# Feed-forward weight tiles loaded block by block into two lasting buffers, and one ordering tie taken out

## The chip, the cores and the metric

The kernel runs on one core of one Trainium2 chip. The metric is the device time of one execution, in microseconds; the time of a kernel is the median of several executions. The profile comes from one further execution that was recorded by the hardware profiler.

## The reference, cut to what matters

One step of a streaming encoder: a convolution layer and an attention layer, each followed by a SwiGLU feed-forward block. Only the two feed-forward blocks are touched by the change. For 640 rows (512 prompt frames and 8 x 16 sample frames), width 1024 and hidden width 2816, each computes

```python
def swiglu_ffn(h, g, w_in, w_out):
    a, b = jnp.split(rms_norm(h, g) @ w_in, 2, axis=-1)
    return h + (jax.nn.silu(a) * b) @ w_out
```

All numbers are float32; the matrix products have to be accurate to about that.

## The kernel before, in words

**Precision.** Every operand x of a product is split into a rounded part "hi" (an ACT copy, line 375) and a rest "lo" (a DVE subtraction, line 376). A product is three matmuls: hi x hi, lo x hi, hi x lo (`product`, line 437, with the matmul on line 444). In the text such a pair of copy and subtraction is a "cut".

**Seven products for eight.** The 640 columns are worked on as two halves of 320, and a weight tile as four blocks. Most tiles (22 inner tiles of a feed-forward block less the first three, and all 12 tiles of the output chunks) replace the eight block products by seven, of sums of blocks (a Strassen scheme). The seven weight operands are called X11, X21, XT2, XT1, XT3, XT4, X22.

**One weight tile** is prepared in `w_seven` (line 414). It takes a buffer `raw` (128 partitions x 2048 floats) from `wraw()` (line 382), which allocates a new tile of a pool with two buffers at each call, so a buffer is free again when everything that touched its last tile is done. One DMA on SP's queue loads the whole tile (line 418): 1024 KB for an inner tile (`w_in`, four blocks of 512 columns), 768 KB for an output tile (`w_os`, four blocks of 384). In the buffer the blocks stand in the order a12, a11, a21, a22, numbered 0 to 3 below. Beside it POOL's queue loads a21 into a small buffer `s1` and then a22 with an accumulating DMA (lines 421 and 422), so that s1 = a21 + a22. Then, in this order for an inner tile:

- X11 is cut from a11, and X21 from a12;
- two DVE sums in place, a21 = a11 + a21 (line 429) and a11 = s1 + a11 (line 430), then XT2 is cut from a11;
- XT1 is cut from s1, XT3 from a21, XT4 from a22;
- a12 = a12 + a11 on DVE (line 432), then X22 is cut from a12.

For an output tile the order is XT1, X11, X21, XT2, X22, XT3, XT4. Each cut goes into one of 11 slots that are taken in turn (line 393), so it waits until the matmuls of the cut eleven places earlier are done.

**The order of the work.** The program is handed to a scheduler, which puts each engine's instructions into a fixed order ahead of time, by priority and its own timeline; at run time each engine works strictly in that order and waits where a semaphore says so. `tc.issue_after(i)` (in the helper `behind`, line 140) forces an instruction behind `i` on the same engine. `w_seven` uses it with `late`: all cuts and sums but those listed in `soon` are put behind the instructions in `late`.

**`seven`** (line 535) does one inner tile: it calls `w_seven`, then the products X11, X21, XT2, XT1, XT3 of this tile, with XT4 and X22 of the tile ahead between them (`before(0)`, `before(1)`). The product X11 is copied out of its accumulator by ACT (`keep`, line 456) before XT2 accumulates on top of it. The list `tile_end` holds the last DVE subtraction of the tile ahead, and is handed to `w_seven` as part of `late` with `soon=(X11, X21, XT1)`: so this tile's sums and its cuts XT2, XT3, XT4, X22 stand behind the last cut of the tile ahead. `chunk_add` does the same with the last addition to h of an output chunk.

**One feed-forward block** (`ffn`, line 337): three inner tiles in the plain way (`w_std`, line 398, which also takes its buffers from `wraw()` and loads them in two DMAs, line 406); then three rounds of inner tiles (3, then 6, then 6) with an output chunk of 4 tiles after each (`out_chunk`, line 568; the order of its products is written out by hand in `QORD`); then four inner tiles; then the rest of the output weights (line 711). The stretch of tiles that go through `w_seven` lasts from about 285 to 625 us in the first block and from about 1050 to 1386 us in the second.

Of the kernel before, what the change touches and what calls it, by code (L numbers as in the profile page):

```python
# [8 lines left out]
F32 = mybir.dt.float32  # L9
# [6 lines left out]
P = 128  # L16
# [44 lines left out]
X11, X21, XT2, XT1, XT3, XT4, X22 = range(7)  # L61
# [24 lines left out]
def tile_trunk(ctx, tc, xT, vecs, hist, w_pw1, w_pw2, w_in0, w_out0, w_os0, w_in1, w_out1, w_os1,  # L86
               w_kq, w_v, w_o, rel, kc, vc, y_out, convp_out, convs_out, k_out, v_out):
    nc = tc.nc

    cst = ctx.enter_context(tc.tile_pool(name="cst", bufs=1))  # L90
    wp = ctx.enter_context(tc.tile_pool(name="wp", bufs=2))
# [12 lines left out]
    def nm(s):  # L104
        uid[0] += 1
        return f"{s}_{uid[0]}"

    def mmt(n=512):
        return mm.tile([P, n], F32, tag="mm", name=nm("mm"))
# [29 lines left out]
    @contextmanager  # L139
    def behind(*ins):  # L140
        with ExitStack() as st:
            for i in ins:
                st.enter_context(tc.issue_after(i))
            yield
# [192 lines left out]
    def ffn(l, w_in, w_out, w_os, tail, hf, lead=(), b0=None, last_sum=()):  # L337
# [19 lines left out]
        lead, put_end = list(lead), [None, None]  # L357

        def ties():
            return lead.pop(0) if lead else ()  # L360
# [13 lines left out]
        def put(hi, lo, src):  # L374
            put_end[1] = nc.scalar.activation(out=hi, in_=src, func=AF.Copy).ins  # L375
            put_end[0] = nc.vector.tensor_tensor(out=lo, in0=src, in1=hi.bitcast(F32), op=sub).ins  # L376

        def cut(w, o, src):
            c = slice(o, o + src.shape[-1])
            put(w[0][:, c], w[1][:, c], src)  # L380

        def wraw():
            return wp.tile([P, 2048], F32, tag="raw", name=nm("raw"))

        wbig = [[wp.tile([P, 2048], F32R, tag="w" + t, name=nm("w" + t)) for t in ("hi", "lo")]
                for _ in range(2)]
# [6 lines left out]
        def slot():  # L393
            turn[0] += 1
            hi, lo, o = slots[(turn[0] - 1) % len(slots)]
            return (hi, lo), o

        def w_std(src, small):
            raw = wraw()
            if small:  # L400
                ws = [slot() for _ in range(3)]
                ws.append(([two(i).rearrange("p a n -> p (a n)") for i in (12, 13)], 0))
            else:
                ws = [slot() for _ in range(4)]
            for i in range(0, 2048, 1024):
                nc.sync.dma_start(raw[:, i:i + 1024], src[:, i:i + 1024])
                with tc.high_priority(offset=HP):
                    n = 512 if small else 1024
                    for j in range(i, i + 1024, n):
                        with behind(*ties()):  # L410
                            cut(*ws[j // 512], raw[:, j:j + n])
            return ws[1], ws[0], ws[2], ws[3]

        def w_seven(src, out=False, first=(), rest=(), late=(), soon=()):
            n = src.shape[-1] // 4
            raw, ws = wraw(), {}
            s1 = wx.tile([P, 512], F32, tag="s1", name=nm("s1"))[:, :n]
            nc.sync.dma_start(raw[:, :4 * n], src)
            a12, a11, a21, a22 = (raw[:, n * i:n * i + n] for i in range(4))
            with tc.high_priority(offset=HP), behind(*ties()):  # L420
                nc.gpsimd.dma_start(s1, src[:, 2 * n:3 * n])  # L421
                nc.gpsimd.dma_start(s1, src[:, 3 * n:4 * n], accum_op=add)
                for x in ((XT1, X11, X21, XT2, X22, XT3, XT4) if out else
                          (X11, X21, XT2, XT1, XT3, XT4, X22)):
                    ws[x] = slot()
                    with behind(*(() if x in soon else late),
                                *(first if x == XT1 else rest)):
                        if x == XT2:
                            nc.vector.tensor_tensor(out=a21, in0=a11, in1=a21, op=add)
                            nc.vector.tensor_tensor(out=a11, in0=s1, in1=a11, op=add)  # L430
                        elif x == X22:
                            nc.vector.tensor_tensor(out=a12, in0=a12, in1=a11, op=add)
                        cut(*ws[x], {XT1: s1, X11: a11, X21: a12, XT2: a11, X22: a12,
                                     XT3: a21, XT4: a22}[x])
            return ws
# [12 lines left out]
        def xproduct(pt, w, x, first):  # L448
            return product(pt, w, [(XH[x][:, k, :], XL[x][:, k, :]) for k in range(4)], first)
# [3 lines left out]
        def keep(tag, pt):  # L453
            t = tp.tile([P, NH], F32, tag=tag, name=nm(tag))
            with tc.high_priority(offset=HP):
                keeps.append(nc.scalar.activation(out=t, in_=pt, func=AF.Copy).ins)  # L456
            return t

        def plus(t, pt):
            with tc.high_priority(offset=HP):  # L460
                nc.vector.tensor_tensor(out=t, in0=pt, in1=t, op=add)

        def silu(t, src):
            with tc.high_priority(offset=HP):
                nc.scalar.activation(out=t, in_=src, func=AF.Silu)  # L465
# [60 lines left out]
                        own(XT4, b21)  # L526
            return sink

        xt2_end, xt3_end, chunk_add, tile_end = [], [None], [], []

        def tie(own):
            xt2_end.append(own)
            return {2: xt2_end[:1], 3: xt2_end[2:]}.get(len(xt2_end), ())

        def seven(src, sink, before):
            ws = w_seven(src, late=chunk_add[:1] + tile_end, soon=(X11, X21, XT1))
            chunk_add[:1], tile_end[:] = (), put_end[:1]
            pa, pb = mmt()[:, :NH], mmt()[:, :NH]
            xproduct(pa, ws[X11], X11, True)
            t1 = keep("t1", pa)  # L540
            before(0)
            xproduct(pb, ws[X21], X21, True)
            plus(t1, pb)
            silu(t1, t1)
            before(1)
            own = xproduct(pa, ws[XT2], XT2, False).ins
            t2 = keep("t2", pa)
            pe = mmt()[:, :NH]
            with behind(*tie(own)):
                xproduct(pe, ws[XT1], XT1, True)  # L550
            xt3_end[0] = xproduct(pa, ws[XT3], XT3, False).ins
            t3 = keep("t3", pa)
            plus(t3, pe)

            def after(i):
                if i == 0:
                    last = xproduct(pa, ws[XT4], XT4, False)
                    sink(0, t1, pa)
                else:
                    last = xproduct(pe, ws[X22], X22, False)  # L560
                    plus(t2, pe)
                    silu(t2, t2)
                    sink(1, t2, t3)
                return last

            return after
# [126 lines left out]
        for c in range(NCH):  # L693
            for jj in range(NSTD if c == 0 else 0, CW):
                if jj % 2 == 0:
                    held = [None] * 3
                if jj == NSTD and c == 0:
                    held = helds[1]
                after = seven(w_in[CW * c + jj], combined(HH, HL, jj // 2, jj % 2, held, True),
                              after)  # L700
            after = out_chunk(c, HH, HL, after)
            HH, HL = {}, {}
        hids = [(two(2 * jj), two(2 * jj + 1)) for jj in range(FT - NCH * CW)]
        for jj, hid in enumerate(hids):
            after = seven(w_in[NCH * CW + jj], plain(hid), after)
# [3 lines left out]
        for m0 in (0, 4):  # L709
            raw, w = wraw(), wbig[m0 // 4]  # L710
            nc.sync.dma_start(raw.rearrange("p (m c) -> p m c", m=4),
                              w_out[m0:m0 + 4].rearrange("m p c -> p m c"))
            with tc.high_priority(offset=HP):
                for o in range(0, 2048, 1024):
                    cut(w, o, raw[:, o:o + 1024])
            done += [(m0 + i, [(w[0][:, b:b + P], w[1][:, b:b + P])
                               for b in range(512 * i, 512 * i + 512, P)]) for i in range(4)]
# [419 lines left out]
    for _ in ffn(0, w_in0, w_out0, w_os0, GR, hf, last_sum=last_sum)[1]:  # L1137
        pass
# [454 lines left out]
    for p in range(NP):  # L1593
# [8 lines left out]
        for op in BO[p].split():  # L1602
# [11 lines left out]
            i = int(op[1]) if len(op) > 1 else None  # L1614
# [25 lines left out]
    adds, late = [], []  # L1640
# [28 lines left out]
    for i in range(SPREAD_AT, KT):  # L1669
        with tc.issue_after(end):  # L1670
# [4 lines left out]

    hf = ExitStack()
    spare, products = ffn(1, w_in1, w_out1, w_os1, ((256, 384), (0, 256)), hf,
                                     [(split_end[0], i) for i in (adds[1], adds[3], eps_end, eps_end)] +
                                     [(eps_end,)],
# [190 lines left out]
```

## Time and profile before

| | us |
|---|---|
| median of 3 runs | 1433.54 |
| lowest, highest | 1432.31, 1435.24 |
| the profiled execution | 1431.13 |
| its span, first to last instruction | 1429.4 |

Engines in the profile: PE is the matrix engine and PEld its loading of weights, which runs beside the matmul ahead; DVE, ACT and POOL are the vector, scalar and general engines; SP issues most DMAs. Their busy times in the span: DVE 1110.7 us, ACT 746.2 us, POOL 280.1 us. A row of the waits names who waited, for whom, the time in total, how often, and the longest. In the rows of instruction groups and of the timeline the brackets or the last columns give the engine's idle time just before, and what ended it. A DMA's row in the chain of waits lasts from its issue until the waiting engine goes on.

### The profile page before, as it was taken

How to read it: one execution, taken by the hardware profiler on the slowest of the kernel's cores; microseconds unless marked ns; L12 is line 12 of the kernel's file. 1: busy time of each engine (PE TensorE's matmuls, PEld its weight loads, DVE VectorE, ACT ScalarE, POOL GpSimd, SP SyncE). 2: the span in 40 equal slices, each digit the busy share in tenths (PEclk: the TensorE clock that was granted, in tenths of full speed). 3: DMA queues.
4: the chain of work that ended last, by engine and by line, in shares of the span. 5: the costliest groups of instructions: out<-in, count | busy, mean ns of one | idle time of the engine just before them, and what ended most of it. 6: DMA issues, size and time to landing. Idle time of an engine off the chain costs nothing.

```text
span 1429.4 us, 28234 instructions
## 1 busy us (share of the span) xinstructions
PE 1416.8 (99%) x11076; PEld 1364.3 (95%) x11076; DVE 1110.7 (78%) x2490; ACT 746.2 (52%) x1633; POOL 280.1 (20%) x335
## 2 busy tenths in 40 slices
PE   9999999999999999999999999999999999999998
PEld 9998799999999999999998988888999999999998
DVE  6799767998888888765666757667899788798765
ACT  5666554554563564545654544544564564465453
POOL 5799120011111111012111111110011111111101
PEclk9999999999999999999999999999999999999999
DMA  7257424054544543524456555561134544543522
GB/s 253 88 168 192 123 84 145 16 137 122 164 112 119 137 123 108 154 89 174 165 187 207 182 185 173 181 215 36 59 99 131 154 127 111 134 131 103 138 86 74
DMA packets 66932, 192.57 MB, mean 135 GB/s; under 512 B 12144, under 2 KB 30320, under 8 KB 58480
## 3 DMA queue, kind: packets, MB, share of 16 engines
q1 hardware_dynamic: 52432, 160.58, 34.4%
q0 software_dynamic: 13504, 29.37, 10.2%
q8 instruction: 87, 1.43, 0.4%
q10 hardware_dynamic: 864, 0.83, 0.2%
q14 instruction: 45, 0.37, 0.1%
HBM read 179.14 MB, written 11.61 MB: 133 GB/s over the span
## 4 chain that ended last, share of the span: by engine, by line
PE 92%; DVE 4%; DMA 1%; ACT 1%; issue 1%; POOL 0%; DVEq 0%; ACTq 0%; POOLq 0%
PE mm L444 51%; PE mm L1304 11%; PE mm L202 6%; PE mm L204 6%; PE mm L203 6%; PE mm L916 3%; PE w L1304 2%; PE am L1477 1%; PE am L1549 1%; PE am L1493 1%; PE w L1448 1%; PE w L1511 1%; DMA raw<-in_w_in 1%; PE mm L149 1%; PE w L243 1%
## 5 line engine op out<-in xcount | busy, mean ns | idle before, releaser
L444 PE MATMUL mm<-XH,whi 128*128 128x320 f32 x896 | 276.2, 310 | 1.3 <-ACT t L456 1.3
L444 PE MATMUL mm<-XH,wlo 128*128 128x320 f32 x896 | 276.5, 309 | 0.0
L444 PE MATMUL mm<-XL,whi 128*128 128x320 f32 x896 | 274.9, 309 | 0.0
L375 ACT ACTIVATE whi<-raw 128x512 fp32r<-128x512 f32 (+2 forms) x280 | 166.7, 613 | 147.4 <-PE mm L444 80.9
L376 DVE TENSOR_TENSOR wlo<-raw,whi 128x512 fp32r<-128x512 f32 (+2 forms) x280 | 185.1, 671 | 23.0 <-ACT whi L375 21.8
L444 PEld LDWEIGHTS mm<-XH,whi 128*128 128x128 f32 x896 | 167.9, 188 | 3.3 <-ACT t L456 3.3
L444 PE MATMUL mm<-hid,whi 128*128 128x320 f32 x732 | 170.9, 310 | 0.2 <-DVE hid L376 0.2
L444 PEld LDWEIGHTS mm<-XH,wlo 128*128 128x128 f32 x896 | 168.2, 188 | 0.0
L444 PEld LDWEIGHTS mm<-XL,whi 128*128 128x128 f32 x896 | 167.8, 188 | 0.0
L202 PE MATMUL mm<-xh,whi 128*128 128x320 f32 (+2 forms) x416 | 128.9, 313 | 0.8 <-DVE h L726 0.4
L203 PE MATMUL mm<-xh,wlo 128*128 128x320 f32 (+2 forms) x416 | 128.1, 310 | 0.0
L444 PEld LDWEIGHTS mm<-hid,whi 128*128 128x128 f32 x732 | 124.7, 188 | 1.8 <-DVE h L595 0.8
L204 PE MATMUL mm<-xl,whi 128*128 128x320 f32 (+2 forms) x416 | 125.5, 310 | 0.0
L595 DVE TENSOR_TENSOR h<-h,mm 128x320 f32<-128x320 f32 x168 | 79.5, 486 | 44.4 <-PE mm L444 44.3
L444 PE MATMUL mm<-hid,wlo 128*128 128x320 f32 x366 | 113.1, 309 | 0.0
L444 PE MATMUL mm<-XH,shi 128*128 128x320 f32 x344 | 105.9, 310 | 0.7 <-DVE h L1581 0.7
L444 PE MATMUL mm<-XH,slo 128*128 128x320 f32 x344 | 106.0, 308 | 0.0
L444 PE MATMUL mm<-XL,shi 128*128 128x320 f32 x344 | 105.7, 309 | 0.0
L872 POOL TENSOR_TENSOR ca<-ca,cvt 128x512 f32<-128x512 f32 x60 | 89.7, 1494 | 15.0 <-ACT cvt L869 8.8
L375 ACT ACTIVATE shi<-raw 128x512 fp32r<-128x512 f32 (+1 forms) x114 | 65.9, 586 | 49.6 <-PE mm L444 21.7
L421 POOL DMA_DIRECT2D s<-in_w_in x38 | 22.0, 580 | 330.4 <-ACT t L465 67.3
L202 PEld LDWEIGHTS mm<-xh,whi 128*128 128x128 f32 x416 | 78.0, 188 | 3.3 <-ACT xh L190 1.5
(337 smaller groups left out, 3662.6 us busy)
## 6 DMA issues: line engine op xcount, KB each, us to landing
raw<-in_w_in SPq DMA_DIRECT2D x38, 1024.0 KB
s<-in_w_in POOLq DMA_DIRECT2D x76, 256.0 KB, 4.2
raw<-in_w_os SPq DMA_DIRECT2D x24, 768.0 KB
cache<-in_ck SPq DMA_DIRECT2D x32, 512.0 KB
cache<-in_cv SPq DMA_DIRECT2D x32, 512.0 KB
raw<-in_w_pw SPq DMA_DIRECT2D x11, 1024.0 KB
s<-in_w_os POOLq DMA_DIRECT2D x48, 192.0 KB, 3.7
raw<-in_w_kq SPq DMA_DIRECT2D x8, 1024.0 KB
```

The lines of the kernel that those rows point to most:

```text
L149: end = nc.tensor.matmul(pt[:, 0:P], ident, ident, start=True, stop=True)
L202: nc.tensor.matmul(ps, wh, xh, start=(first and i == 0), stop=False)
L203: nc.tensor.matmul(ps, wl, xh, start=False, stop=False)
L204: end = nc.tensor.matmul(ps, wh, xl, start=False, stop=(stop and i == last))
L375: put_end[1] = nc.scalar.activation(out=hi, in_=src, func=AF.Copy).ins
L376: put_end[0] = nc.vector.tensor_tensor(out=lo, in0=src, in1=hi.bitcast(F32), op=sub).ins
L421: nc.gpsimd.dma_start(s1, src[:, 2 * n:3 * n])
L444: last = nc.tensor.matmul(pt, wt, v, start=(first and k == i == 0), stop=(k == n - 1 and i == 2), skip_group_check=True)
L595: hadd[i, u] = [nc.vector.tensor_tensor(out=hv, in0=hv, in1=pt, op=sub if row else add).ins]
L872: nc.gpsimd.tensor_tensor(out=acc, in0=acc, in1=pr, op=ALU.add)
L916: conv_end[0] = nc.tensor.matmul(pt[32 * q:32 * q + 32, 0:n], w4[0:r, 4 * tg + q, :], mv, start=(tg == 0), stop=(tg == 7)).ins
L1304: step_end[0] = nc.tensor.matmul(ps, w, x, start=i == j == 0, stop=i == len(wts) - 1 and j == 2).ins
```

## The change

Three things, all in `ffn`:

- Two buffers `raw` are allocated once for the whole feed-forward block and used in turn, so what a new load has to wait for is decided by the parts of the buffer that were read or written, and no longer by the whole of its last tile. Beside each buffer stands an order of its four blocks.
- In `w_seven` the one load becomes four, of a block each, all on SP's queue. The blocks of an output tile now start 512 columns apart too. The first load of a buffer through `w_seven` goes in the order 0, 1, 2, 3; a load after an inner tile in the order 2, 3, 1, 0 (a21, a22, a11, a12); a load after an output tile in the order 1, 0, 2, 3.
- The list `tile_end` is gone: the sums and later cuts of an inner tile are put behind `chunk_add` only.

```diff
+        raws = [[wp.tile([P, 2048], F32, tag="raw", name=nm("raw")), (0, 1, 2, 3)]
+                for _ in range(2)]
+
         def wraw():
-            return wp.tile([P, 2048], F32, tag="raw", name=nm("raw"))
+            raws.reverse()
+            return raws[1][0]
...
             raw, ws = wraw(), {}
+            blocks = [raw[:, 512 * i:512 * i + n] for i in range(4)]
             s1 = wx.tile([P, 512], F32, tag="s1", name=nm("s1"))[:, :n]
-            nc.sync.dma_start(raw[:, :4 * n], src)
-            a12, a11, a21, a22 = (raw[:, n * i:n * i + n] for i in range(4))
+            for i in raws[1][1]:
+                nc.sync.dma_start(blocks[i], src[:, n * i:n * i + n])
+            raws[1][1] = (1, 0, 2, 3) if out else (2, 3, 1, 0)
+            a12, a11, a21, a22 = blocks
...
-        xt2_end, xt3_end, chunk_add, tile_end = [], [None], [], []
+        xt2_end, xt3_end, chunk_add = [], [None], []
...
-            ws = w_seven(src, late=chunk_add[:1] + tile_end, soon=(X11, X21, XT1))
-            chunk_add[:1], tile_end[:] = (), put_end[:1]
+            ws = w_seven(src, late=chunk_add[:1], soon=(X11, X21, XT1))
+            chunk_add[:1] = ()
```

## The prediction

> **What bounds the kernel now.** I read the page first, then busy times by stretches of the two places that the change touches, then the waits of PE's weight loads there, and last the chain of waits and the timeline around the worst gap.
>
> ```profile
> PE 1416.8 (99%) x11076; PEld 1364.3 (95%) x11076; DVE 1110.7 (78%) x2490; ACT 746.2 (52%) x1633; POOL 280.1 (20%) x335
> PE mm L444 51%; PE mm L1304 11%; PE mm L202 6%; PE mm L204 6%; PE mm L203 6%; PE mm L916 3%; PE w L1304 2%; PE am L1477 1%; PE am L1549 1%; PE am L1493 1%; PE w L1448 1%; PE w L1511 1%; DMA raw<-in_w_in 1%; PE mm L149 1%; PE w L243 1%
> ```
>
> PE is the bound, and half of the chain that ended last is matmuls of line 444, those of the feed-forward blocks. The change takes away no matmul, so it can win only the time in which PE stands still. How much is that where the tiles go through `w_seven`? The two stretches, and the waits of PEld in them (first the two rows of the first block, then the three of the second):
>
> ```profile
> 285.00:625.00 340.00, 339.71 (x2306) 337.88 (x2306) 284.63 (x575) 178.75 (x367) 40.89 (x57) 1.00 0.46 127
> 1050.00:1386.00 336.00, 334.78 (x2263) 331.55 (x2262) 279.19 (x567) 174.56 (x362) 40.18 (x56) 1.00 0.46 128
> ...
> PEld mm L444 <- ACT t L456: 0.7, 3, 0.2
> PEld mm L444 <- DVE h L595: 0.5, 3, 0.2
> ...
> PEld mm L444 <- ACT t L456: 2.6, 6, 0.7
> PEld mm L444 <- DVE h L595: 0.9, 4, 0.3
> PEld mm L444 <- DVE hid L376: 0.4, 1, 0.4
> ```
>
> The columns of the first two rows are the stretch and its length, then the busy time and count of PE, PEld, DVE, ACT and POOL, the granted clock, the DMA share and GB/s. The clock is 1.00 in both, so it explains nothing. All the waits together are 0.7 + 0.5 + 2.6 + 0.9 + 0.4 = 5.1 us: **the most that this change can bring is about 5 us of 1433.54, 0.36%.** The two blocks run the same code, yet the first takes 340/2306 = 147.4 ns per matmul and the second 336/2263 = 148.5 ns. At the first one's pace the second would be 1.03 ns x 2263 = 2.3 us shorter. That is a second, nearer bound: what the first block loses are six waits of about 0.2 us, two in each of its three rounds, and no load stands in them.
>
> Where is a load behind a gap? The chain of waits around 1251 us, in the second block:
>
> ```profile
> 1232.89 0.64 ACT whi L375
> ...
> 1233.56 0.70 DVE wlo L376
> ...
> 1234.28 4.99 DMA raw<-in_w_in
> ...
> 1243.58 7.54 DMA raw<-in_w_in
> ...
> 1251.20 0.13 ACT whi L375
> ...
> 1251.74 0.45 ACT t L465
> 1252.19 0.33 ACT t L456
> ...
> 1252.57 1.44 PE mm L444 x8
> ```
>
> A load is issued only when the last cut of the buffer's last tile is done (1233.56, then the DMA at 1234.28), and nothing of the tile can start until all of it has landed. At 1243.58 that came too late. The timelines of ACT and PE show how a load that PE does not wait for stops it:
>
> ```profile
> 1251.20 0.63 ACT L375 ACTIVATE whi<-raw 128x512 fp32r<-128x512 f32 x1 [3.48 <-DMA raw<-in_w_in]
> 1251.74 0.45 ACT L465 ACTIVATE t<-t 128x320 f32<-128x320 f32 x1
> 1252.10 0.42 ACT L456 ACTIVATE t<-mm 128x320 f32<-128x320 f32 x1
> ...
> 1251.63 0.31 PE L444 MATMUL mm<-XL,whi 128*128 128x320 f32 x1
> 1251.77 0.31 PE L444 MATMUL mm<-XH,whi 128*128 128x320 f32 x1
> 1252.57 0.42 PE L444 MATMUL mm<-XH,whi 128*128 128x320 f32 x1 [0.48 <-ACT t L456]
> 1252.82 0.32 PE L444 MATMUL mm<-XH,wlo 128*128 128x320 f32 x1
> ```
>
> ACT stood 3.48 us in front of the first cut of the new tile; behind it in ACT's order was the copy of an accumulator (line 456) that PE needs back. Matmuls start 0.14 us apart before the gap, 0.80 us across it and 0.25 us after it: it costs 0.80 - 0.14 + 0.25 - 0.14 = 0.77 us, rounded from rows of two digits.
>
> **The change part by part.** *Loads in blocks.* Each of the 62 tiles (38 and 24 below) gets three more DMAs on SP, so 186 issues of 0.33 us.
>
> ```profile
> raw<-in_w_in SPq DMA_DIRECT2D x38, 1024.0 KB
> raw<-in_w_os SPq DMA_DIRECT2D x24, 768.0 KB
> L418 SPq DMA_DIRECT2D raw<-in_w_in x38: 327/328/328, 243.8 to 1355.2; - x38
> SPq L418 <- DVE wlo L376: 569.3, 50, 42.0
> SPq L418 <- DVE slo L376: 127.4, 12, 13.5
> ```
>
> That is 61 us of SP's time, on a queue that waits 569.3 + 127.4 = 697 us for cuts to be done (all 62 loads wait for one), and that carries nothing else in these stretches but the next tile: nothing on the path. What does a load of a block cost the DMA engines? The kernel's first tiles already come in pieces of this size:
>
> ```profile
> raw<-in_w_pw SPq DMA_DIRECT2D x8, 256.0 KB
> 5.00:10.00 5.00, 5.00 (x37) 5.00 (x37) 4.12 (x10) 2.69 (x6) 0.00 (x0) 1.00 1.02 360
> 1000.00:1005.00 5.00, 5.00 (x36) 5.00 (x36) 4.77 (x7) 4.98 (x10) 0.00 (x0) 1.00 0.63 210
> ```
>
> With these pieces in flight the engines moved 360 GB/s at a share of 1.02, which is 353 for a full share; the second row, at the second block's first whole-tile loads, has 210 at 0.63, 333 for a full share. So I charge the split at nothing in rate. The Trainium skill says otherwise: its page "DMA: Bandwidth & Descriptors", section "Rules for kernel authors", asks for at least 1 MiB per DMA and for small transfers to be put together, which speaks straight against a split into 256 KB. The row at 5 us does not bear it out for DMAs queued behind each other; by the page alone the sum would have a loss in it, a rival below.
>
> *When a load starts and when its first use can.* X11, the first cut, needs block a11 alone. Now, after an inner tile, a21 and a22 go out as soon as XT3 and XT4 are cut, a11 after the sum of line 432, and only a12 still waits for the last cut. Of the 1024 KB, a quarter stands behind the old moment of issue instead of all, and X11 waits for none of that quarter. Of the load's 7.54 us at 1243.58 at least the part that the other three blocks take goes; ACT was 3.48 us late, PE lost 0.77. I take the whole gap: **-0.77 us**. The same way round, the other waits on loads shrink:
>
> ```profile
> ACT whi L375 <- DMA raw<-in_w_in: 17.6, 12, 3.5
> ACT whi L375 <- DMA raw<-in_w_os: 12.8, 5, 2.8
> ACT shi L375 <- DMA raw<-in_w_in: 10.4, 8, 2.2
> ```
>
> They are 40.8 us in 25 waits, 1.63 us each; but the gap above is the one that I can trace to PE, so taking them away is worth nothing more at once. ACT then waits for what comes next, the slot to write into, and that costs PE nothing either.
>
> *The tie.* Without it the sums of lines 429 and 430 may go ahead of the last cuts of the tile ahead. The work is the same: three DVE sums per tile, 0.64 us each by line 429's row below. What it can bring is a better filled DVE at the start of a round, where DVE is full and PE waits for `hid`:
>
> ```profile
> 1050.00:1060.00 10.00, 9.62 (x66) 9.36 (x65) 8.32 (x16) 5.49 (x12) 1.45 (x2) 1.00 0.63 169
> 1070.00:1080.00 10.00, 9.85 (x67) 9.53 (x66) 10.00 (x24) 5.28 (x12) 1.46 (x2) 1.00 0.62 169
> L429 DVE TENSOR_TENSOR raw<-raw 128x512 f32<-128x512 f32 (+1 forms) x62 | 39.4, 636 | 2.1 <-DMA raw<-in_w_os 1.2 <-DMA raw<-in_w_in 0.9
> ```
>
> DVE is idle for 1.68 us from 1050 to 1060 and full from 1070 on. Two sums moved from the full part into the empty one (1.3 us) would take the wait for `hid` (0.4 us) and perhaps the 0.4 us by which the waits for line 595 exceed those of the first block. From below, nothing, if the scheduler leaves the order as it is, or a loss (the second rival); from above, 0.8 us. I take the middle, **-0.4 us**, since the slots hold the cuts themselves back in any case. The 2.3 us bound allows both terms.
>
> *What I can't cost* is what the scheduler makes of freer loads in its fixed order, on PE too. Its bounds are the 5.1 us below and the second rival above; I take 0.
>
> **Sum:** -0.77 - 0.4 = -1.2 us. On the profiled execution's own time 1431.13 (span 1429.4 and 1.7 around it) that is 1429.9. The median of the runs lies 2.4 us above the profiled execution, so the forecast on the median is 1433.54 - 1.2 = **1432.3 us**. About 0.2%, 2.9 us, is what a measurement of this kernel can tell from no change; this is less.
>
> **The rivals.** *Faster.* The earlier loads take nearly all of PE's waits: 1433.54 - 5.1 = 1428.4. Against it: the 0.7 + 0.5 us of the first block are short waits for copies and additions to h behind PE's own products, and the second block has as many of them. To pass 0.2% more than half of all must go. Chance 0.12.
>
> *Slower: DVE stops in front of loads.* Line 429 needs a11 and a21. Tied, it came late, and waited for a load 2.1 us in all. Untied, the scheduler may set it right behind the moment at which it believes the blocks to be there; if they are later, DVE stands still, with every subtraction and accumulator read behind it, just as ACT stood at 1251. DVE has 676 - 563.8 = 112 us of room in the two stretches, 1.8 us per tile, and a wait like ACT's takes 1.63. Where DVE is full, that goes on to PE. At the one measured price, 0.77 us, ten such tiles of 62 cost 7.7: 1432.3 + 7.7 = 1440.0. It decides from (2.9 + 1.2)/0.77, six tiles, on. For it speaks how little room DVE has; against it, that the blocks now land earlier too. Chance 0.16.
>
> *The change does nothing*: SP's queue is in order, a21 is waited for first, and if XT3's cut comes late in DVE's order all four blocks go out together where the one did. Then the time stays 1433.5. Chance 0.17.
>
> *Slower: small loads.* If four blocks were paid for one after the other, at the 4.2 us of the nearest row, a tile would take 16.8 us to load against 12.3 us of matmuls (seven products of 4 x 3, 84, at 0.147), and 38 inner tiles alone would add 38 x 4.5 = 171 us: 1604. This is what the skill's rule on 1 MiB would come to at worst; the 360 GB/s speak against it. Chance 0.02.
>
> ```profile
> s<-in_w_in POOLq DMA_DIRECT2D x76, 256.0 KB, 4.2
> ```
>
> **How the numbers follow.** The forecast has 0.53, doing nothing 0.17; of the forecast's I give 0.04 to faster by over 0.2% (the 2.3 us bound and the spread of the runs) and 0.01 to slower. So faster is 0.12 + 0.04 = 0.16, slower 0.16 + 0.02 + 0.01 = 0.19, same 0.65. The range goes from the lower bound, 1428.4, to seven waits of the second rival, 1432.3 + 7 x 0.77 = 1437.7; left out are the second rival's worse half and the last one, about 1 in 10.
>
> **What would show it.** Right, if ACT's waits for raw loads fall from 40.8 us to under 15, the gap of 0.8 us in front of a matmul waiting for line 456 behind a load is gone, four loads of a block stand for each tile with 300 to 360 GB/s per full share, and the second stretch needs about 147.8 ns per matmul. Wrong, if DVE waits at line 429 for loads by more than 10 us (second rival), or if PEld's waits in the two stretches are under 2 us (first) or over 8 us.

## The result, and the profile after

The changed kernel takes 1441.41 us (median of 6 runs, 1439.61 to 1441.6); the kernel before, in the same number of runs, 1432.72. The ratio is 1.0057, 95% interval 1.0047 to 1.0067: slower by 8 us, outside the range. The profiled execution took 1441.38 us, its span is 1439.6, and the granted clock is 1.0.

In the numbers of the changed kernel all lines from 418 on lie lower: the loads are on 424, the sums on 436, 437 and 439 (before: 429, 430, 432), the matmul on 451, the copy of an accumulator on 463, two accumulator reads of DVE on 468 and 602.

The page, its engines, its chain of work by engine and the issues of the raw loads:

```profile
PE 1419.1 (99%) x11076; PEld 1363.7 (95%) x11076; DVE 1109.9 (77%) x2490; ACT 744.3 (52%) x1633; POOL 279.8 (19%) x335
...
PE 80%; DVE 12%; DMA 4%; issue 2%; ACT 2%; POOL 0%; DVEq 0%; ACTq 0%; POOLq 0%
...
raw<-in_w_in SPq DMA_DIRECT2D x152, 256.0 KB
...
raw<-in_w_os SPq DMA_DIRECT2D x96, 192.0 KB
```

The chain by engine in the kernel before:

```profile
PE 92%; DVE 4%; DMA 1%; ACT 1%; issue 1%; POOL 0%; DVEq 0%; ACTq 0%; POOLq 0%
```

Four loads stand for each tile. The engines do the same number of instructions, and DVE is busy for 0.8 us less than before. But the chain that ended last, 92% PE's and 4% DVE's before, now runs through DVE for 12% of the span and through transfers for 4%. The waits of the trace, those of DVE and of ACT for the raw loads:

```profile
DVE raw L436 <- DMA raw<-in_w_in: 42.7, 19, 3.9
...
ACT whi L375 <- DMA raw<-in_w_in: 24.3, 10, 3.1
...
ACT shi L375 <- DMA raw<-in_w_in: 8.3, 4, 3.0
...
DVE raw L437 <- DMA s<-in_w_in: 4.8, 6, 1.9
```

The first sum waited for loads 2.1 us in all before; now it waits 42.7 us, up to 3.9 us at a time. ACT's waits fell from 40.8 to 32.6 us only: those for output tiles are gone, those for inner tiles grew from 28.0 us. What this does to PE, in busy times by stretches; the first row is of the kernel before (three plain tiles and the first tiles of the scheme), the three of the other fence are of the changed kernel:

```profile
230.00:285.00 55.00, 55.00 (x385) 55.00 (x384) 48.64 (x113) 29.22 (x62) 0.64 (x1) 1.00 0.15 54
```

```profile
230.00:285.00 55.00, 53.35 (x371) 53.09 (x371) 46.70 (x109) 28.23 (x60) 0.41 (x1) 1.00 0.21 64
285.00:625.00 340.00, 337.00 (x2277) 333.60 (x2276) 280.98 (x573) 173.78 (x363) 40.90 (x58) 1.00 0.49 126
1050.00:1386.00 336.00, 333.87 (x2257) 330.84 (x2257) 281.27 (x574) 173.64 (x362) 41.43 (x58) 1.00 0.50 127
```

PE does 14, 29 and 6 matmuls fewer in the same stretches. 49 of them at 0.147 us are 7.2 of the 10.2 us between the two spans; most is lost in the first block. One more microsecond is a gap of PE at 169 us, in code that the change doesn't touch. PE's own waits in the stretch from 285 to 625 us, and the chain of work at the longest of them:

```profile
PEld mm L451 <- DVE t L468: 2.8, 2, 1.8
PEld mm L451 <- DVE h L602: 0.9, 3, 0.5
PEld mm L451 <- ACT t L463: 0.8, 3, 0.3
PEld mm L451 <- ACT whi L375: 0.6, 2, 0.4
PEld mm L451 <- DVE wlo L376: 0.5, 1, 0.5
PEld mm L451 <- ACT shi L375: 0.4, 1, 0.4
```

```profile
391.55 0.62 DVE wlo L376
...
392.19 5.63 DMA raw<-in_w_in
...
397.91 0.69 DVE raw L436
398.60 0.40 DVE B L491
...
400.32 0.48 DVE B L491
400.81 0.41 DVE t L468
```

The timelines of DVE and of PE at the same place:

```profile
397.91 0.69 DVE L436 TENSOR_TENSOR raw<-raw 128x512 f32<-128x512 f32 x1 [3.88 <-DMA raw<-in_w_in]
...
400.72 0.48 DVE L468 TENSOR_TENSOR t<-mm,t 128x320 f32<-128x320 f32 x1
```

```profile
399.26 0.31 PE L451 MATMUL mm<-XL,whi 128*128 128x320 f32 x1
399.40 0.31 PE L451 MATMUL mm<-XH,whi 128*128 128x320 f32 x1
401.26 0.41 PE L451 MATMUL mm<-XH,whi 128*128 128x320 f32 x1 [1.55 <-DVE t L468]
401.52 0.31 PE L451 MATMUL mm<-XH,wlo 128*128 128x320 f32 x1
```

Read it forwards: the last cut of an old tile ends, the load into the freed block (a11 of the new tile, the last of its four to leave) is issued at 392.19, DVE comes to the new tile's sum at 394.03 (397.91 less 3.88) and stands there until the block is in. Behind the sum, in DVE's fixed order, come a few short operations and then the accumulator read of line 468, which PE needs before it can go on. Matmuls start 1.86 us apart across the gap, where 0.14 is usual, and 0.26 after it: 1.84 us lost of a wait of 3.88. About 2 us of this wait are covered by work that PE already has. The cover isn't the same everywhere: DVE's wait of 2.62 us at 253.8 holds up the small operations on the norm's statistics, and PE stands for 1.81 us behind them.

The gap at 1251.77 us of the kernel before is gone. In its place PE has one of 0.80 us at 1246.9, behind a sum that waited 3.32 us, and behind ACT, which stood 3.01 us in front of X11's cut for the same block, a11.

Where do the long waits stand? Two rows of DVE's timeline:

```profile
367.39 0.69 DVE L436 TENSOR_TENSOR raw<-raw 128x512 f32<-128x512 f32 x1 [2.79 <-DMA raw<-in_w_in]
...
369.05 0.69 DVE L436 TENSOR_TENSOR raw<-raw 128x512 f32<-128x512 f32 x1
```

The first is the sum of the third inner tile of a round, the second that of the second tile (each sum was paired with the loads of its own two blocks, from the built program and the trace). The scheduler has put the third tile's sum ahead of the second's. DVE comes to it 0.76 us after its block a11 was issued, and stands, while the blocks of the second tile have been in for 11 us. This happens behind each output chunk, six times in all, with waits of 2.65 to 3.32 us. In the last of six inner tiles, four times, DVE comes to the sum 1.8 us after the issue and waits 2.15 to 3.88 us. These are ten of the 13 waits over 2 us. In the kernel before the sums stand in the tiles' order, and DVE comes to none of them sooner than 4.07 us after its load's issue.

### The profile page after: what moved, and what is told of

It is laid out like the page before. It is cut to its first block, busy times and chain, and to the rows that moved or that the text cites. A ratio compares the mean times of both kernels' runs of the same rounds, so it can differ in the third digit from the quotient of the medians.

```text
span 1439.6 us, 28730 instructions
## 1 busy us (share of the span) xinstructions
PE 1419.1 (99%) x11076; PEld 1363.7 (95%) x11076; DVE 1109.9 (77%) x2490; ACT 744.3 (52%) x1633; POOL 279.8 (19%) x335
## 4 chain that ended last, share of the span: by engine, by line
PE 80%; DVE 12%; DMA 4%; issue 2%; ACT 2%; POOL 0%; DVEq 0%; ACTq 0%; POOLq 0%
PE mm L451 41%; PE mm L1311 10%; PE mm L202 5%; PE mm L204 5%; PE mm L203 5%; DMA raw<-in_w_in 3%; PE mm L923 3%; DVE wlo L376 2%; PE w L1311 2%; PE am L1484 1%; PE am L1556 1%; PE am L1500 1%; PE w L1455 1%; PE w L1518 1%; DVE slo L376 1%
## 5 line engine op out<-in xcount | busy, mean ns | idle before, releaser
L879 POOL TENSOR_TENSOR ca<-ca,cvt 128x512 f32<-128x512 f32 x60 | 89.6, 1493 | 17.1 <-ACT cvt L876 10.9
```

The costliest lines, as they stand in the source:

```text
L879: nc.gpsimd.tensor_tensor(out=acc, in0=acc, in1=pr, op=ALU.add)
```

## The experiments

The theory after reading this trace (A in the expectations): the untied first sum stands in front of its load, and everything behind it on DVE is late. Against it: the four loads cost by themselves (B); the scheduler's new order costs by itself, whatever the waits (C). On why the blocks are late: POOL's accumulating load moves at the same time (D), a landing is mostly a fixed time whatever the size (E), or a11 stands too late in the queue (F).

All ratios are to the kernel before, on the same chip.

**Each half alone.** The changed kernel with the tie put back:

```diff
-            ws = w_seven(src, late=chunk_add[:1], soon=(X11, X21, XT1))
-            chunk_add[:1] = ()
+            ws = w_seven(src, late=chunk_add[:1] + tile_end, soon=(X11, X21, XT1))
+            chunk_add[:1], tile_end[:] = (), put_end[:1]
```

> The changed kernel with the tie alone put back (blocks and lasting buffers stay). Theory A: the untied first sum stands in DVE's order ahead of its load, DVE waits for raw loads at that sum 42.7 us in 19 waits, and PE pays. Then DVE's waits for raw loads fall under 10 us and the time is 1431 to 1435. Theory B: the blocks themselves are the loss, a block of 256 KB lands hardly sooner after its issue than the tile of 1024 KB did and a11 is only third in the queue; then the tie changes little and the time stays at 1438 to 1442. Theory C: any change of the scheduler's order costs about this much; then it lies anywhere from 1430 to 1442 and the DVE waits say nothing about it.

Measured: 0.9997 (0.9988 to 1.0006). The row of DVE's waits:

```profile
DVE raw L436 <- DMA raw<-in_w_in: 1.1, 2, 0.9
```

The whole loss is gone with the waits, so four loads into lasting buffers cost nothing, and B falls; they bring nothing either.

The kernel before with the tie taken out (the same diff the other way round), its loads whole:

> The kernel before with the tie alone taken out (one load of a whole tile). Theory A: the sums now wait in DVE's order for a load of 1024 KB; DVE's waits at the first sum are 30 us or more and the time is 1438 to 1443. Theory B: no blocks, so no loss, 1431 to 1435. Theory C: anywhere.

Measured: 0.9993 (0.9983 to 1.0002), and the waits:

```profile
DVE raw L429 <- DMA raw<-in_w_in: 7.7, 8, 2.4
```

So the missing tie alone doesn't cost anything: a miss for A as it was put. Only both together are slow. A whole load can't be issued before the last cut of the old tile, and the scheduler sets the sum late enough behind it. From the issue of the last block that the first sum needs until DVE comes to that sum there are 10.4 us in the kernel before (median of 62 tiles), 7.9 here, 6.8 in the changed kernel, with 25 of its tiles under 4 us (one here, none before). The load itself takes 5.2, 5.3 and 3.4 us of it. Here too the sums stand in the tiles' order.

Four loads in the buffers of the kernel before, a new one for each tile, with the tie:

```diff
-            nc.sync.dma_start(raw[:, :4 * n], src)
-            a12, a11, a21, a22 = (raw[:, n * i:n * i + n] for i in range(4))
+            a12, a11, a21, a22 = (raw[:, 512 * i:512 * i + n] for i in range(4))
+            for i, a in ((1, a11), (0, a12), (2, a21), (3, a22)):
+                nc.sync.dma_start(a, src[:, n * i:n * i + n])
```

> The kernel before with four loads of a block into buffers of the pool (all four wait until the whole buffer is free), in the order a11, a12, a21, a22; the tie stays. Theory A: the sums are tied, so no loss: 1431 to 1435. Theory B: all four blocks go out at the moment of the old load, each DMA pays for its issue, the last block lands later than the old load did and the time is 1436 or more.

Measured: 1.0019 (1.0008 to 1.0029), a third of the loss, with 8.9 and 3.9 us of waits at the first sum, and one gap of PE of 2.2 us at 317 us. That gap stands behind ACT, which waited 3.39 us for POOL's load of `s1` in front of a cut; so it isn't shown that this loss comes from the sum.

**Why the blocks are late, with the order held.** In the next three kernels the order of DVE's and PE's instructions is that of the changed kernel, or differs from it in at most one per cent of the places, so only the loads differ. POOL's second load of `s1` overwrites:

```diff
-                nc.gpsimd.dma_start(s1, src[:, 3 * n:4 * n], accum_op=add)
+                nc.gpsimd.dma_start(s1, src[:, 3 * n:4 * n])
```

> The changed kernel, every engine's instructions in the same order, but POOL's second load into s1 overwrites instead of accumulating (s1 is then a22, not a21 + a22: XT1 and XT2 get wrong weights). Only what the transfers do to each other changes. Theory D: the scheduler sets the first sums 2.8 to 4.6 us after the last block's issue, and the blocks land too late for that because they share the DMA engines with POOL's accumulating load; then the blocks land sooner, DVE's waits at the first sum fall from 42.7 us to under 20 and the time to 1432 to 1437. Theory E: a block's landing is late by itself, by the fixed time of a DMA; then the waits stay at 35 to 45 us and the time at 1439 to 1443.

Measured: 1.0030 (1.0018 to 1.0043). That second load left out altogether (the `-` line alone):

> The changed kernel without POOL's second, accumulating load into s1 (s1 is then a21 alone: XT1 and XT2 get wrong weights); the order of the engines' instructions is nearly that of the changed kernel. If sharing the DMA engines with POOL's loads is a good half of the price, as with the plain second load (1436.6), leaving it out altogether gives 1433 to 1436, with DVE's waits at the first sum at 25 to 36 us. If the accumulation itself was the disturbance and not the bytes, the same as with the plain load, 1436 to 1438.

Measured: 1.0015 (1.0003 to 1.0026). The waits of the two kernels:

```profile
DVE raw L436 <- DMA raw<-in_w_in: 36.6, 19, 3.3
```

```profile
DVE raw L435 <- DMA raw<-in_w_in: 37.5, 19, 3.7
```

The sum of the waits falls only by 5 or 6 us, the loss by about half or more. The waits in the last of six inner tiles get shorter: they were 2.15 to 3.88 us, and are 1.36 to 2.23 with the overwriting load and 1.40 to 1.62 with none. PE's waits for line 468 behind them, 2.8 and 0.3 us in the two stretches of the changed kernel, are gone in both. The six sums that stand ahead of another tile's wait as long as ever, 2.8 to 3.5 us. So a part of the loss comes from POOL's accumulating load beside SP's (D, in part). The place of a11 in the queue:

```diff
-            raws[1][1] = (1, 0, 2, 3) if out else (2, 3, 1, 0)
+            raws[1][1] = (1, 0, 2, 3) if out else (1, 2, 3, 0)
```

> The changed kernel, compute engines in the same order, but after an inner tile the blocks are loaded in the order a11, a21, a22, a12 instead of a21, a22, a11, a12. Theory F: a11's third place in SP's queue is what makes the first sum late; then DVE's waits at it fall by half or more and the time is 1434 to 1438. Theory E or D: a11 is free only after the last sum of the buffer's last tile, and a21, which the first sum needs too, now stands behind it; then nothing is won: 1440 to 1444, waits of 40 us or more.

Measured: 1.0054 (1.0042 to 1.0066), waits of 42.0 us in 20. This is no test of F. The scheduler orders SP's queue too, and the program built from this edit is that of the changed kernel, instruction for instruction: in both, a11 leaves third in 30 of the 38 inner tiles, second in four and last in four. (So the orders named with the change are those in which the loads are written; an inner tile behind an output tile leaves as 3, 2, 1, 0.) The run is the changed kernel measured once more, and shows how well it repeats: 1.0054 and 1.0057, 42.0 us and 42.7, 11 and 13 waits over 2 us. F stays open.

**The sum elsewhere.** Behind the subtraction of its own tile's X21, still untied:

```diff
-                            nc.vector.tensor_tensor(out=a21, in0=a11, in1=a21, op=add)
+                            with behind(*(() if out else put_end[:1])):
+                                nc.vector.tensor_tensor(out=a21, in0=a11, in1=a21, op=add)
```

> The changed kernel, still without the tie to the tile ahead, but the first sum of an inner tile is put behind the subtraction of X21 of its own tile, which needs block a12, the last to be loaded. Theory A: the sum can no longer be the first instruction on DVE to meet its load; DVE's waits at it fall to about 0, and the time is 1432 to 1436. If it is the tie to the tile ahead as such that matters (its last cuts first), the time stays at 1438 to 1442. Theory B: 1438 to 1442.

Measured: 1.0018 (1.0008 to 1.0028). Inner tiles' sums wait no more, and nearly all of the loss is now one place, where ACT stands in front of a load. From the chain of work:

```profile
1049.68 5.43 DMA raw<-in_w_in
...
1055.19 0.63 ACT whi L375
1055.82 0.34 ACT t L464
...
1056.20 1.99 PE mm L452 x8
```

The same behind X11's subtraction instead, one cut earlier:

> The changed kernel, untied, with the first sum of an inner tile behind the subtraction of X11 of its own tile: that one needs block a11 too, so the sum stands behind another instruction that has met the load, but the tie to the tile ahead is still gone and a12 need not be there. Theory A: DVE's waits at the first sum fall to under 5 us and the time to 1431 to 1436, wherever ACT does not take over the wait in front of X11; if it does, one gap of PE per place where ACT waits for more than 3 us. If the cuts ahead of the tile ahead are what costs, 1438 to 1442.

Measured: 1.0041 (1.0027 to 1.0055), also without a wait of an inner tile's sum for its load. Its loss is in other waits of PE:

```profile
PEld mm L454 <- DVE h L605: 6.5, 12, 1.0
...
PEld mm L454 <- ACT t L466: 3.9, 4, 2.2
```

The sum on POOL instead of DVE (`nc.gpsimd.tensor_tensor`), in the changed kernel:

> The changed kernel with the first sum of each tile on POOL instead of DVE (still without the tie). Theory A: what the sum waits for no longer stops DVE; DVE's waits for raw loads fall under 5 us, 40 us of DVE work are gone, and the time is 1429 to 1434, at best better than both kernels. Against: POOL needs about 1.5 us where DVE needs 0.64, and POOL's own loads of s1 stand behind the waiting sum; if that is what counts, ACT and DVE wait for s1 instead, and the time is 1436 to 1445.

and with whole loads, in the kernel without the tie:

> The kernel before without the tie (as tie_off, one load for a whole tile), with the first sum of each tile on POOL. If DVE's load is what PE still waits for, 1428 to 1431; if POOL's loads of s1 behind the sum come late, 1434 to 1445.

Measured: 1.0172 (1.0155 to 1.019) and 1.0201 (1.0187 to 1.0214). The groups of instructions of the first of them:

```profile
L376 DVE TENSOR_TENSOR wlo<-raw,whi 128x512 fp32r<-128x512 f32 (+2 forms) x280 | 194.6, 709 | 28.5 <-ACT whi L375 27.9
...
L436 POOL TENSOR_TENSOR raw<-raw 128x512 f32<-128x512 f32 (+1 forms) x62 | 93.4, 1507 | 143.2 <-DMA raw<-in_w_in 53.3 <-DMA raw<-in_w_os 49.0 <-DVE wlo L376 19.1
...
L437 DVE TENSOR_TENSOR raw<-s,raw 128x512 f32<-128x512 f32 (+1 forms) x62 | 40.1, 646 | 24.1 <-DMA s<-in_w_in 24.0
```

POOL needs 1507 ns in the mean for what DVE does in 636, and the sum waits in POOL's order ahead of POOL's own loads: DVE now waits 24.0 us for `s1` in front of the second sum. It was no way to take the wait away.

**Two loads of two blocks**, untied and tied, each into lasting buffers:

```diff
-            for i in raws[1][1]:
-                nc.sync.dma_start(blocks[i], src[:, n * i:n * i + n])
+            for i in ((0, 2) if out else (2, 0)):
+                nc.sync.dma_start(raw[:, n * i:n * i + 2 * n], src[:, n * i:n * i + 2 * n])
```

> The changed kernel, untied, but a tile in two loads of two blocks each (after an inner tile a21 and a22 together, then a12 and a11) instead of four. If the loss comes from how much too early the scheduler sets the first sum for a load of this size, the halves lie between whole tiles untied (DVE waits at the first sum 9 us, time as before) and quarters (42.7 us, 1441): 15 to 35 us of waits and 1433 to 1439. If any split of the load without the tie costs the same, 1440 to 1443; if only the number of DMAs on SP counts, a third of the loss, 1434 to 1435.

> The same two loads in lasting buffers with the tie kept. Candidate for a version better than both kernels: DVE's waits at the first sum under 4 us, and ACT's waits for raw loads (30.4 us in front of line 375 for inner tiles and 12.8 for output tiles before) fall as the loads start earlier: 1429 to 1432. If ACT's waits do not reach PE anyway, 1431 to 1434, no difference.

Measured: 1.0038 (1.0027 to 1.0049) and 1.0046 (1.0029 to 1.0063). The first is as expected, with 17.1 and 4.7 us of waits at the first sum. The second is a miss: tied, it has hardly a wait of DVE in front of a raw load (3.5 and 0.9 us), and loses as much. Its largest waits of PE:

```profile
PEld mm L450 <- ACT t L462: 8.3, 12, 1.5
```

In the kernel before this row has 3.8 us in 10 waits. Loads may have a part here too: ACT stands 24.5 us in front of raw loads in this kernel (40.8 before), and PE's wait at 368.6 us comes straight behind one of them, while its wait at 480.97 us has no load in the chain. So a loss of 0.4% nearly without DVE's waits is shown, its cause is not; C may hold for this order.

**Waits or order, in the changed kernel?** The loads of a tile after the first of each buffer cut to a half and to an eighth, with POOL's second load overwriting:

```diff
+                m = n if raws[1][1] == (0, 1, 2, 3) else n // 2
-                nc.sync.dma_start(blocks[i], src[:, n * i:n * i + n])
+                nc.sync.dma_start(blocks[i][:, :m], src[:, n * i:n * i + m])
```

> As the kernel with eighths, with loads cut to a half, 128 KB (the weights are wrong here too). Between the run with whole blocks and overwriting (36.6 us of waits, ratio 1.003) and that with eighths, in waits and in time, if the waits cause the loss; at 1.002 to 1.004 whatever the waits, if the order does.

> The changed kernel with POOL's second load of s1 overwriting, as in the run before that had that alone, and besides every load of a block after the first of each buffer cut to its first eighth, 32 KB; the rest of the block keeps old numbers, so the weights of the tiles are wrong. The order of DVE's instructions stays as in the changed kernel but for 188 of 2492, nearer to it than the tied kernel's. If the remaining loss is that of DVE waiting for loads, the wait at line 436 for raw loads falls from 36.6 us to under 15 and the ratio from 1.003 to 1.0005 or less. If it is the order of the work, the waits fall as well and the ratio stays at 1.002 to 1.004. If a block's landing is a fixed time that its size hardly changes, the waits stay over 25 us, and the time says nothing.

Measured: 0.9978 (0.9966 to 0.999) and 0.9978 (0.9968 to 0.9988), with these waits:

```profile
DVE raw L437 <- DMA raw<-in_w_in: 19.1, 17, 3.5
```

```profile
DVE raw L437 <- DMA raw<-in_w_in: 15.6, 10, 4.2
```

The waits are those of the halves, then of the eighths. They didn't fall under 15 us, but the loss is not only gone, it has turned round. Is that the untied order, paid back at last, or the quick loads? The kernel with halves, with the tie:

> The kernel with halved loads (128 KB, POOL's second load of s1 overwriting, so the weights of the tiles are wrong), with the tie put back. That kernel without the tie took 0.9978 of the time of the kernel before, although DVE still waited 19.1 us at the first sum. If untied sums are worth something as soon as their loads come in time, this one, tied, gives 0.9990 to 1.0005 with waits under 2 us there. If it is the halved loads alone that are faster, it gives 0.9970 to 0.9985.

Measured: 0.9979 (0.997 to 0.9988), with one wait of a sum for a raw load, of 0.3 us. With halved loads, tied and untied are equal; with whole blocks (and POOL's load accumulating) they differ by 0.6%. The order with halves isn't quite the changed kernel's: 119 of DVE's 2490 instructions stand elsewhere, and PE's matmuls differ in 737 of 11076 places (in the kernel with the tie back, 1398). But the six sums ahead of another tile's are there, at the same 0.76 us behind their loads; DVE waits 1.75 to 1.82 us at each, and nothing is lost. So the order without the tie costs nothing by itself there, and gives nothing: **its loss is that its loads are late for it**. The 0.2% below the kernel before comes with smaller loads (and POOL's plain ones) under either order, and is not to be had with all the weights.

Waits of DVE's sums for loads, raw and `s1`, counted in DVE's timeline:

| | over 2 us | all, us | ratio |
|---|---|---|---|
| changed kernel | 13 | 47.5 | 1.0057 |
| a11 first (the same program) | 11 | 44.2 | 1.0054 |
| without POOL's second load | 9 | 37.5 | 1.0015 |
| POOL's second load overwriting | 8 | 37.4 | 1.0030 |
| halves | 1 | 20.8 | 0.9978 |
| eighths | 1 | 16.9 | 0.9978 |
| before, tie off | 1 | 9.3 | 0.9993 |
| changed kernel, tie back | 0 | 2.1 | 0.9997 |
| four loads, new buffers, tied | 3 | 14.1 | 1.0019 |
| sum behind X21 | 0 | 1.4 | 1.0018 |
| sum behind X11 | 0 | 5.4 | 1.0041 |
| two loads | 3 | 29.4 | 1.0038 |
| two loads, tied | 1 | 7.3 | 1.0046 |

In the first six rows, whose order is the changed kernel's or near it, the loss goes with the long waits: 21 us in short ones cost nothing that can be measured. The same program twice gives 13 and 11, so 9 and 8 are not told apart, and the intervals of these two kernels overlap. The last five rows have other orders and don't follow: they lose 0.2 to 0.5% with few long waits or none, for the reasons above or for none that is shown.

## Why the prediction was wrong, point by point

**The bound** was right as a bound on the gain, though 5.1 us is a little small: the row of the first block leaves out a fourth wait, of 0.5 us, at 624.6 us. For the whole stretch it reads

```profile
PEld mm L444 <- ACT t L456: 1.2, 4, 0.5
```

and the bound is 5.6 us. It is none on a loss, and the change's danger lay there. (The 147.8 ns per matmul named as a sign should be 148.0: 148.5 less 1.2 us over 2263 matmuls. It came to 336/2257 = 148.9.)

**Loads in blocks, priced at nothing in rate.** Right in effect, wrong in the number: 126 GB/s at a share of 0.49 are 257 for a full share, where whole loads have 127 at 0.46, 276. Nothing hung on it at a share of one half: with the tie back the kernel with four loads takes 0.9997 of the time. The rate is 7% lower, in the direction of the Trainium skill's rule ("DMA: Bandwidth & Descriptors", section "Rules for kernel authors"), which asks for at least 1 MiB per DMA. The 300 to 360 that I named as a sign didn't come even for whole loads.

**When a first use can start.** Here the first step failed. I took it that a block, a quarter of the load, is in soon. Read from the semaphores of the trace, a whole inner tile landed 5.2 us after its issue (median), a block 3.7. A quarter of the bytes bought 1.5 us; an eighth of a block (32 KB) still takes 1.79 us, so by these medians a large part of a block's landing doesn't go with its size (E). And a11 did not leave as early as I had it, "after the sum of line 432": the cut of XT2 reads it too, and DVE does that cut behind this sum. Behind an inner tile a11 left 0.8 to 4.4 us ahead of a12, and in the last of six inner tiles after it, as at 392.19. ACT's waits for the raw loads of inner tiles didn't shrink: 28.0 us before, 32.6 now. The row for the landing stood in the prediction, POOL's 256 KB at 4.2 us from issue to landing, beside a whole load at 4.99 in the chain; I used it for the rate of a queue and not for the delay. The −0.77 us did come, in that the gap at 1251.77 is gone, and was lost again at 1246.9.

**The tie, taken as "the middle, -0.4 us", between nothing and 0.8.** This is the term that failed most: with blocks, taking out the tie cost 8.6 us (0.6% between the changed kernel and the one with the tie back). The text names the loss, "or a loss (the second rival)", and then leaves it out of the middle. Without blocks it is worth nothing that can be measured, so the gain I put on a better filled DVE isn't there.

**The second rival came true**: DVE stops at the first sum's load, 42.7 us against the 10 that I gave as its sign; PE's waits in the two stretches, by the six rows above and five like them (4.8 us) in the second block, are 10.8 us against the 8; the time is 1441.4 against 1440.0. Ten tiles at 0.77 us were not quite the way there: 13 waits over 2 us, of which few reach PE, and those cost up to 1.8 us. What I set against it, "that the blocks now land earlier too", did not help: with the loads earlier and the tie gone the scheduler set the sum earlier still, 6.8 us behind the issue instead of 10.4 in the median and 0.76 us in the worst six, where a load needs 3.4 us to land. That it goes by the time at which it believes a block to be in is argued from this, not shown. The range left out this rival's worse half, and so ended below the result.

**The other rivals.** "Does nothing" failed, since the order moved. "Faster" had its room, but the loads that would take it aren't quick enough; with halved loads the time fell by 0.2%, about 3 us. The small loads' price of 4.2 us one after the other is not what four loads in a queue pay: with the tie back they cost nothing.

Open is what remains in kernels where the scheduler's order differs: two loads with the tie, and the sum behind X11, lose 0.4% in waits for copies and for additions to h, and no run here separates that from the size of their loads. Open too is whether an a11 that really leaves first would help (F), and what a tie that only keeps the sums in the tiles' order would give; no run has either.

## What to carry to other kernels

On an engine that works in a fixed order, ask of each instruction that gets freer what it will now meet: its data in time, or a load that it waits for with everything behind it; a tie that looks like a needless delay can be the margin that covers a load. Then look at the order that came out: here a sum stood in front of its load while another's data had been in for 11 us, and an edit to the order of the loads left the built program as it was. A load cut in four is not there in a quarter of the time, so price its delay from a row of that size before moving its first use forward. And where two edits meet (earlier loads, freer users), price them together: each alone was worth nothing here, and both cost 0.6%.

## What the runs showed of the hardware that was not expected

Landings of SP's loads (median, own reading from the semaphores): 1.79 us for 32 KB, 2.44 for 128 KB, 3.52 for 256 KB, all three with POOL's plain loads beside them; 3.67 for 256 KB with POOL's accumulating load; 5.17 for 1024 KB in the kernel before. The Trainium skill, "DMA: Bandwidth & Descriptors", section "Anatomy of one DMA — SWDGE (gpsimd) path", gives about 2.0 us that don't depend on the size, and bytes at 436 GB/s on top, for loads issued by GpSimd. SP's loads here agree in kind: 32 KB, an eighth of a block, still take half of a block's time; 1024 KB would by it be an estimated 4.4 us and took 5.17.

A sum on POOL slowed DVE down: the subtractions of line 376, with both inputs in SBUF, went from 668 to 709 ns in the mean, while the additions of line 602, which read an accumulator, took 482 ns and then 481. Of the subtractions on `raw` of 128x512, the 29 that ran beside a sum on POOL took 975 ns in the mean, the other 133 took 684. The Trainium skill, "SBUF — State Buffer", section "Who interferes with whom", says just this: a DVE instruction with two SBUF inputs contends with a GpSimd instruction that reads SBUF, one with at most one SBUF input, outside DVE's two-port modes, doesn't.
